# A two-layer mixture-of-experts backbone: experts in a pipelined order, their weights in longer runs, and a reordered routing chain

## Chip, cores and metric

One core of a Trainium2 chip runs the whole program in one launch. The metric is the device time of that launch in microseconds (us), as the median of several runs. TensorE is PE in the profile, VectorE DVE, ScalarE ACT, GpSimd POOL, SyncE SP; SP issues the weight transfers.

## What is computed

Two layers over 256 latent and 256 context tokens of 1024 channels, all in f32. Each layer has a token mixer (differential attention, a long convolution called hyena, windowed attention; gated and merged) and then a mixture of 16 experts in which every expert chooses its tokens:

```python
def moe(h, p):                     # h: (B, L, D), per sequence
    aff = softmax(h @ router_w)    # over the 16 experts
    g, idx = top_k(aff.T, CAP)     # each expert takes its CAP = 2 * 256 / 16 = 32 best tokens
    xe = gather(h, idx)            # (E, CAP, D)
    a = silu(xe @ moe_w1[e]) * (xe @ moe_w3[e])
    y = a @ moe_w2[e]              # all three 1024 x 1024
    return scatter_add(g * y, idx)
```

In layer 0 latent and context tokens are two sequences (64 rows to an expert); layer 1 needs the latent ones alone (32 rows). h is a normalized x, scaled and shifted per channel by values that the conditioning vector gives (`mod`, vectors 3 and 4 here). Each layer reads 3 x 16 x 4 MB = 201 MB of expert weights, once.

## The kernel before

Stages follow one another: mixer of layer 0 (about 60 to 950 us), routing, experts of layer 0 (1030 to 1515), mixer of layer 1 (1545 to 2145), routing, experts of layer 1 (2165 to 2621), final norm.

**Foreground and background.** `run_blocks` issues a list of projection blocks; each block's matmuls are the foreground. What follows from them (attention heads, hyena, filter, modulation, router, `post`) are generators, called tasks, kept by `self.bg`, a planner with a model of the engines' time. It steps tasks between foreground matmuls, by rough costs and due times, and `drain` or `force` run them without foreground. `yield wait(..., gate=...)` holds a task until its gate is true; `self.room(a2=2)` is a gate that asks for two dead buffers of the tag a2 (8 buffers of 2 KB to a partition). Allocating a tile of a full tag makes the engines wait for its old readers.

**Routing** (`post` for each of 8 channel tiles k, then `body` in `moe`). `post` transposes xT tile by tile to token rows and splits them into three bf16 parts xr[0], xr[1], xr[2] (through the difference tile xd), and accumulates the router's logits. Then come the softmax aff, four rounds of MAX and MATCH_REPLACE on a copy wk of its transpose, the mask's running count (mt, mb16), and `select(g)`, which builds one-hot matrices S for a group of 4 experts. `gather(g)` makes the experts' inputs xg out of S and xr in four steps of 24 matmuls; R is the row norm spread over the partitions; mod[:, 4] and mod[:, 3] scale and shift.

**Experts.** The weights come in 96 chunks of 2 MB for each layer, 6 to an expert (w1, w3, w2, two halves each), into 6 or 7 large buffers and a few smaller ones ahead of time. `fill(room)` (line 1622) issues as many as there is room for, on SP; `prod` (line 1786) calls it whenever it has used up a chunk (4 of the 8 k-steps; a k-step is 2 matmuls in layer 0, 4 in layer 1). `expert(e)` (line 1800) runs its three products one after the other: a = x w1, SiLU to s1, b = x w3, s1 = s1 * b, then transposes of s1 to aT, then y = aT w2. Into the k-steps `aside()` mixes steps of the side queue (gather and back of the next group, scatter of the last) and `bg.pump` background tasks. In layer 0 after expert 4 the room falls to 4 chunks, since layer 1's hyena filter takes buffers. PSUM has 5 banks of tag b and 2 of tag d (y).

In chunks, partition p holds rows p, 128 + p, ...: `v = A[n][l, e].rearrange("(k p) n -> p k n", p=128)`, a run of 4 KB for each row.

## Time and profile before

| | us |
|---|---|
| runs (3), median | 2635.15 |
| lowest and highest run | 2632.49, 2641.01 |
| the profiled execution, its time | 2637.57 |
| the profiled execution, its span | 2635.8 |

Busy in that span: PE 2232.3 us (85%), DVE 1334.5 (51%), ACT 883.4 (34%), POOL 790.4 (30%). 590.31 MB were moved, 224 GB/s on the mean. A window view gives for each stretch the span's busy time by engine, the granted clock of PE, the busy share of the 16 DMA engines (packets that overlap can take it over 1) and GB/s. In a row of a group view the time after the bar is idle time of that engine just before the group's instructions, and the releaser that ended most of it.

### The profile page before, as it was taken

The page shows a single profiled execution, that of the slowest core. Times are in us where ns is not written, and L with a number is a line of the kernel's source. Part 1 is how long each engine was busy: PE and PEld are TensorE (multiplying, and loading weights), DVE is VectorE, ACT ScalarE, POOL GpSimd, SP SyncE. Part 2 cuts the span into 40 slices and gives each one's busy share as a digit, 9 for nine tenths or more (in the row PEclk, how much of TensorE's full clock was granted, in tenths as well). Part 3 has the DMA queues.
Part 4 walks back from the last instruction along what each step waited for, and adds up shares of the span by engine and source line. Part 5 has one row for each costly group of instructions (what it writes and reads, how often), then busy time and mean ns, then how long its engine had stood idle before and what let it go on. Part 6 is the DMA issues. An engine that isn't in the chain of part 4 may idle for free.

```text
span 2635.8 us, 38658 instructions
## 1 busy us (share of the span) xinstructions
PE 2232.3 (85%) x14938; PEld 1528.6 (58%) x14938; DVE 1334.5 (51%) x2899; ACT 883.4 (34%) x1933; POOL 790.4 (30%) x775
## 2 busy tenths in 40 slices
PE   6999898989989998998999799889888886656565
PEld 4777666767768774333343277777777763222223
DVE  4777778787672324223442068777888541111111
ACT  4445344555452242101110055545545330000001
POOL 2643435532233530001110055564554420000000
PEclk8999999999999999999999999999999988888887
DMA  8444333121213367999999953332466789999997
GB/s 292 118 118 120 93 102 114 49 59 55 64 57 95 90 247 306 373 402 404 357 376 405 400 171 89 97 88 73 118 181 190 192 309 409 409 409 409 408 409 302
DMA packets 390239, 590.31 MB, mean 224 GB/s; under 512 B 45948, under 2 KB 278056, under 8 KB 388776
## 3 DMA queue, kind: packets, MB, share of 16 engines
q1 hardware_dynamic: 390056, 587.84, 62.8%
q8 instruction: 118, 1.93, 0.3%
q14 instruction: 65, 0.53, 0.1%
HBM read 584.66 MB, written 3.15 MB: 223 GB/s over the span
## 4 chain that ended last, share of the span: by engine, by line
PE 51%; DVE 19%; DMA 19%; issue 4%; ACT 4%; SPq 2%; POOL 1%; DVEq 0%; ACTq 0%; POOLq 0%
PE p L458 47%; DMA mw<-in_moe_w_dram 16%; DVE arena L261 6%; DVE t L261 5%; PE p L469 3%; DVE wl L261 2%; SPq L261 2%; DMA wm<-in_w_mod_dram 2%; DVE qp L261 1%; ACT arena L261 1%; ACT wh L261 1%; DVE yb L261 1%; DVE yc L261 1%; DVE ma L261 1%; POOL wl L261 1%
## 5 line engine op out<-in xcount | busy, mean ns | idle before, releaser
L458 PE MATMUL p<-mw,xg 128*32 128x256 f32 (+1 forms) x3072 | 403.3, 508 | 120.5 <-DMA mw<-in_moe_w_dram 120.0
L458 PE MATMUL p<-hhi,wl 128*128 128x512 f32 (+1 forms) x1344 | 480.6, 358 | 28.0 <-DVE wl L261 27.7
L458 PE MATMUL p<-hhi,wh 128*128 128x512 f32 (+1 forms) x1344 | 496.0, 369 | 6.4 <-ACT wh L261 3.3
L458 PE MATMUL p<-hlo,wh 128*128 128x512 f32 (+1 forms) x1344 | 476.6, 355 | 2.5 <-POOL hlo L261 1.3
L261 POOL TENSOR_TENSOR wl<-wraw,wh 128x512 fp32r<-128x512 f32 x232 | 342.4, 1476 | 417.5 <-ACT wh L261 344.8
L458 PEld LDWEIGHTS p<-mw,xg 128*32 128x32 f32 (+1 forms) x3072 | 136.3, 131 | 329.6 <-issue 205.4
L458 PEld LDWEIGHTS p<-hhi,wl 128*128 128x128 f32 x1344 | 258.4, 192 | 76.1 <-DVE wl L261 41.7
L458 PEld LDWEIGHTS p<-hhi,wh 128*128 128x128 f32 x1344 | 259.4, 193 | 43.6 <-issue 10.1
L458 PEld LDWEIGHTS p<-hlo,wh 128*128 128x128 f32 x1344 | 259.6, 193 | 29.5 <-POOL hlo L261 1.9
L261 ACT ACTIVATE wh<-wraw 128x1024 fp32r<-128x1024 f32 x232 | 242.3, 1053 | 54.0 <-DMA wraw<-in_w_in_dram 14.7
L458 PE MATMUL p<-mw,aT 128*32 128x256 f32 (+3 forms) x1760 | 199.5, 469 | 67.8 <-DMA mw<-in_moe_w_dram 51.6
L261 DVE TENSOR_TENSOR wl<-wraw,wh 128x512 fp32r<-128x512 f32 x231 | 196.2, 850 | 79.4 <-ACT wh L261 73.9
L261 ACT ACTIVATE arena<-p 128x512 f32<-128x512 f32 (+1 forms) x212 | 106.7, 506 | 383.0 <-PE p L458 304.9
L261 ACT ACTIVATE yS<-p 32x256 f32<-32x256 f32 (+2 forms) x84 | 35.2, 419 | 497.3 <-PE p L458 463.8
L458 PE MATMUL p<-yb,wh 128*128 128x512 f32 (+1 forms) x768 | 197.3, 347 | 1.4 <-ACT wh L261 1.2
L261 POOL TENSOR_TENSOR sq<-sq,sq 128x512 f32<-128x512 f32 (+1 forms) x6 | 6.3, 1058 | 575.6 <-ACT sq L261 573.3
L458 PEld LDWEIGHTS p<-mw,aT 128*32 128x32 f32 (+1 forms) x1760 | 77.1, 131 | 172.9 <-issue 92.7
L261 DVE TENSOR_TENSOR s<-s,p 128x512 f32<-128x512 f32 (+1 forms) x32 | 17.7, 554 | 287.6 <-PE p L458 287.4
L261 DVE COPY yS<-p 32x512 f32<-32x512 f32 (+1 forms) x60 | 33.3, 556 | 247.1 <-ACT yS L261 247.1
L458 PE MATMUL p<-yb,wl 128*128 128x512 f32 (+1 forms) x384 | 133.3, 347 | 22.5 <-DVE wl L261 21.6
L458 PEld LDWEIGHTS p<-yb,wh 128*128 128x128 f32 x768 | 133.3, 194 | 17.3 <-ACT wh L261 1.4
L261 ACT ACTIVATE arena<-p,t 128x512 f32<-128x512 f32 (+1 forms) x192 | 116.3, 612 | 50.9 <-DVE t L261 45.7
(235 smaller groups left out, 3489.7 us busy)
## 6 DMA issues: line engine op xcount, KB each, us to landing
mw<-in_moe_w_dram SPq DMA_DIRECT2D x173, 2048.0 KB, 19.5
wraw<-in_w_in_dram SPq DMA_DIRECT2D x152, 512.0 KB, 3.9
wm<-in_w_mod_dram SPq DMA_DIRECT2D x72, 512.0 KB, 4.7
mw<-in_moe_w_dram SPq DMA_DIRECT2D x40, 512.0 KB, 15.8
mw<-in_moe_w_dram SPq DMA_DIRECT2D x17, 1024.0 KB, 22.4
wraw<-in_w_branch_dram SPq DMA_DIRECT2D x32, 512.0 KB, 3.9
wm<-in_w_mod_dram SPq DMA_DIRECT2D x5, 2048.0 KB, 7.7
wraw<-in_w_in_dram SPq DMA_DIRECT2D x32, 256.0 KB, 3.3
```

Of the source, the lines that this page charges most:

```text
L261: return f(*args, **kw)
L458: self.nc.tensor.matmul(out, lhsT=lhsT, rhs=rhs, start=start, stop=stop, skip_group_check=tiles > 1)
L469: self.nc.tensor.transpose(out, in_, self.ident[:n, :n])
```

## The change

**Chunks.** w1 and w3 now give partition p the rows 8p to 8p + 7, so that half a matrix is a run of 16 KB to a partition; w2 gives it nf neighbouring rows in each part (nf = 4 in layer 0: 16 KB, nf = 2 in layer 1: 8 KB). The extra chunks that fill small buffers keep runs of 4 KB, twelve later chunks of layer 1 are split into one run of 8 KB and two of 4 KB, and the last expert's w2 stays as it was. To match, `post` writes xr with its columns permuted (channel 8p + k to place 128k + p in the gather's order), s1 is transposed with stride nf, and `router_prep` permutes vectors 3 and 4 of mod by 8 matmuls against selections of the identity matrix.

**Order of experts.** The chunk order is (0,w1), (0,w3), then for each e: (e+1,w1), (e,w2), (e+1,w3). `into(e, n)` is a first or second product, `turned(e)` the transposes and aT, `outof(e)` the third product. `turned(e)` is called in the middle of the next expert's first product.

**Routing.** The last `post` hands its xd, xr[1], xr[2] to `self.rest`, called behind the normalization of aff; MAX reads the transpose in PSUM (no copy wk); the cast to mb16 comes ahead of mt; the matmuls and the copy of R come ahead of the gather of k = 1; after two of the four gather steps of group 0 the first product begins, with the other two steps between its k-steps. Gather and back of the next group are queued one expert earlier.

**Gates.** Waits of filter and router get gates on a2; `clear(n)` forces background until n buffers of a2 are dead; hyena's uh and ul are allocated a step earlier, and yc once for two.

```diff
@@ router_prep
         if v == 4:
-            yield wait(self.modc[l][:, 4])
+            yield wait(self.modc[l][:, 4], gate=self.room(a2=2))
             self.router_prep(l)
...
+        m = self.modc[l][:, 3:5]
+        p = self.bank([128, KT, 2 * KT * 2])
+        for hf in range(2):
+            sw = self.sb("a2", [128, 4, KT, 16], name="sw")
+            self.vcopy(sw, self.ident.rearrange("p (q c) -> p c q", c=KT)[:, hf * 4:hf * 4 + 4, None, :].to_broadcast([128, 4, KT, 16]))
+            for c in range(4):
+                self.mm(p[:, hf * 4 + c], sw[:, c].rearrange("p k q -> p (k q)"), m.rearrange("p v k s -> p (v k s)"), True, True)
...
+        nc.vector.reduce_sum(own, self.ident.rearrange("p (k q) -> p k q", k=KT), axis=AX.X)
...
+        nc.vector.reduce_sum(m.rearrange("p v c s -> p c v s"), t.rearrange("p (c v) k s -> p c v s k", v=2), axis=AX.X)
@@ filter
-            yield wait(ab[0])
+            yield wait(ab[0], gate=self.room(a2=1))
...
-                yield wait(w3, dec) if j else wait()
+                yield wait(w3, dec) if j else wait(gate=self.room(a2=1))
...
+    def clear(self, n):
+        while self.model.dead("a2", BUFS["a2"]) < n:
+            self.bg.force()
@@ post
-        self.acopy(xr[0], p)
-        self.tt(d, p, xr[0], OP.subtract)
-        self.acopy(xr[1], d)
-        self.tt(xr[2], d, xr[1], OP.subtract, self.nc.gpsimd)
+        self.acopy(xr[0], pv)
+
+        def rest():
+            self.tt(d, pv, xr[0], OP.subtract)
+            self.acopy(xr[1], d)
+            self.tt(xr[2], d, xr[1], OP.subtract, self.nc.gpsimd)
+
+        if k < KT - 1:
+            rest()
+        else:
+            self.rest = rest
@@ moe
         for e in range(NE):
-            for n in ("moe_w1", "moe_w3", "moe_w2"):
-                v = A[n][l, e].rearrange("(k p) n -> p k n", p=128)
...
+            order += [(e + 1, 0), (e, 2), (e + 1, 1)] if e < NE - 1 else [(e, 2)]
...
+                        v = A[n][l, e].rearrange("(c p j) n -> p c j n", p=128, j=nf)
+                        chunks.append(v[:, hf * NC // 2:(hf + 1) * NC // 2])
+                else:
+                    chunks.append(A[n][l, e].rearrange("(p k) n -> p k n", p=128)[:, hf * 4:hf * 4 + 4, :])
...
             self.tt(aff, aff, mb, OP.mult)
+            self.rest()
...
-            wk = self.sb("a1", [E2, 256], name="wk")
-            self.vcopy(wk, p[0:E2])
+            wk = p[0:E2]
...
-            def prod(out, st, ws, free=True):
+            def prod(out, st, ws, free=True, mid=None):
...
-                    if k % SIDE or not aside():
+                    if mid and k == 4:
+                        mid()
+                    elif k % SIDE or not aside():
                         self.bg.pump(0.25)
...
+            def into(e, n, mid=None):
                 g, j = divmod(e, 4)
                 a = self.bank([128, N])
-                prod(a, st, w[0:2])
-                s1 = self.sb("a2", [128, N], name="s1")
-                nc.scalar.activation(s1, a, AF.Silu)
-                b = self.bank([128, N])
...
+                prod(a, lambda k: xg[g][k // 4][:, k % 4, j, :], weights(e, n), mid=mid)
...
+            def turned(e):
+                s1 = s1s.pop(e)
                 p = self.bank([128, nf, 128])
                 for f in range(nf):
-                    self.tr(p[:, f], s1[:, f * 128:(f + 1) * 128])
...
+                    self.tr(p[:, f], s1[:, f::nf] if e < NE - 1 else s1[:, f * 128:(f + 1) * 128])
...
-            finish(gather(0))
+            side.append(gather(0))
+            for _ in range(2):
+                aside()
+            into(0, 0)
...
-                if j == 2 and g < 3:
+                if j == 1 and g < 3:
                     side += [gather(g + 1), back(g + 1)]
...
-                expert(e)
+                into(e, 1)
+                if e < NE - 1:
+                    if j == 3:
+                        while aside():
+                            pass
+                    into(e + 1, 0, lambda: turned(e))
+                else:
+                    turned(e)
+                outof(e)
```

**What this moves.** First DVE, in the routing of layer 0, from the softmax (t is a small tile, aff the affinities) to the first MATCH_REPLACE. Before:

```order
L261 SCALAR_TENSOR_TENSOR t_8783<-t_8804,t_8802 128x4
L261 TENSOR_TENSOR xd_8774<-p_8767,xr_8373 128x512
L261 SCALAR_TENSOR_TENSOR aff_403<-p_8816,t_8783,cr_2951 128x16 x2
L261 SCALAR_TENSOR_TENSOR aff_403<-p_8817,t_8783,cr_2951 128x16 x2
L261 TENSOR_REDUCE t_8826<-aff_403 128x4
L261 TENSOR_TENSOR aff_403<-aff_403,t_8826 128x64
L261 TENSOR_REDUCE t_8826<-aff_403 128x4
L261 RECIPROCAL t_8826<-t_8826 128x4
L261 TENSOR_TENSOR aff_403<-aff_403,t_8826 128x64
L261 COPY wk_8866<-p_8863 32x256
L261 MAX t_8868<-wk_8866 32x8
L261 MATCH_REPLACE wk_8870<-t_8868,wk_8866 32x256
```

And after:

```order
L261 SCALAR_TENSOR_TENSOR t_8793<-t_8814,t_8812 128x4
L261 SCALAR_TENSOR_TENSOR aff_403<-p_8823,t_8793,cr_2977 128x16 x2
L261 SCALAR_TENSOR_TENSOR aff_403<-p_8824,t_8793,cr_2977 128x16 x2
L261 TENSOR_REDUCE t_8833<-aff_403 128x4
L261 TENSOR_TENSOR aff_403<-aff_403,t_8833 128x64
L261 TENSOR_REDUCE t_8833<-aff_403 128x4
L261 RECIPROCAL t_8833<-t_8833 128x4
L261 TENSOR_TENSOR aff_403<-aff_403,t_8833 128x64
L261 TENSOR_TENSOR xd_8784<-p_8777,xr_8383 128x512
L261 MAX t_8876<-p_8873 32x8
L261 MATCH_REPLACE wk_8878<-t_8876,p_8873 32x256
```

The difference xd went from ahead of the affinities to behind them, and the copy wk is gone.

Then PE, in layer 0's experts: products of expert 0 up to its third one (p is the PSUM bank, mw a chunk, xg the gathered input, s the s1 of the text). Before:

```order
L458 MATMUL p_9090<-mw_8402,xg_8935 64x512 x8
L458 MATMUL p_9090<-mw_8455,xg_8936 64x512 x8
L458 MATMUL p_9113<-mw_8508,xg_8935 64x512 x8
L458 MATMUL p_9113<-mw_8561,xg_8936 64x512 x8
L469 MATMUL p_9135<-cst_68,s_1499_9111 128x128 x4
L458 MATMUL p_9142<-mw_8904,aT_9140 64x512 x2
L458 MATMUL p_9142<-mw_8905,aT_9140 64x512 x2
L458 MATMUL p_9142<-mw_8906,aT_9140 64x512 x2
L458 MATMUL p_9142<-mw_8907,aT_9140 64x512 x2
L458 MATMUL p_9142<-mw_8912,aT_9140 64x512 x8
```

And after, from expert 0's second product on:

```order
L458 MATMUL p_9121<-mw_8518,xg_8943 64x512 x8
L458 MATMUL p_9121<-mw_8571,xg_8944 64x512 x8
L458 MATMUL p_9143<-mw_8912,xg_8943 64x512 x2
L458 MATMUL p_9143<-mw_8913,xg_8943 64x512 x2
L458 MATMUL p_9143<-mw_8914,xg_8943 64x512 x2
L458 MATMUL p_9143<-mw_8915,xg_8943 64x512 x2
L458 MATMUL p_9143<-mw_8920,xg_8944 64x512 x2
L469 MATMUL p_9154<-cst_68,s_1495_9107 128x128 x4
L458 MATMUL p_9143<-mw_8920,xg_8944 64x512 x6
L458 MATMUL p_9171<-mw_8922,aT_9159 64x512 x8
```

p_9143 is expert 1's first product: the transposes of expert 0's s1 went into its middle, with ten of its matmuls ahead of them and six behind.

## Rows read from the trace of the kernel before

**Rows 1.** The page's busy times, and GB/s in its 40 slices.
```profile
PE 2232.3 (85%) x14938; PEld 1528.6 (58%) x14938; DVE 1334.5 (51%) x2899; ACT 883.4 (34%) x1933; POOL 790.4 (30%) x775
...
GB/s 292 118 118 120 93 102 114 49 59 55 64 57 95 90 247 306 373 402 404 357 376 405 400 171 89 97 88 73 118 181 190 192 309 409 409 409 409 408 409 302
```

**Rows 2.** Windows: length, PE, PEld, DVE, ACT, POOL busy; PEclk, DMA, GB/s.
```profile
60.00:950.00 890.00, 833.31 (x4508) 645.20 (x4507) 596.12 (x1300) 402.80 (x881) 384.90 (x382) 0.98 0.31 91
1030.00:1510.00 480.00, 426.18 (x2132) 163.19 (x2128) 136.57 (x310) 58.44 (x130) 36.68 (x65) 0.99 0.99 387
2170.00:2605.00 435.00, 265.10 (x3107) 121.31 (x3099) 49.75 (x126) 25.38 (x70) 0.00 (x0) 0.84 1.03 409
```

**Rows 3.** The page's chain that ended last, by line.
```profile
PE p L458 47%; DMA mw<-in_moe_w_dram 16%; DVE arena L261 6%; DVE t L261 5%; PE p L469 3%; DVE wl L261 2%; SPq L261 2%; DMA wm<-in_w_mod_dram 2%; DVE qp L261 1%; ACT arena L261 1%; ACT wh L261 1%; DVE yb L261 1%; DVE yc L261 1%; DVE ma L261 1%; POOL wl L261 1%
```

**Rows 4.** Windows in transfers: 8 KB loads, 16 KB spill, its reload, 4 KB expert weights.
```profile
18.00:20.00 2.00, 1.15 (x2) 0.30 (x2) 1.86 (x6) 0.00 (x0) 0.00 (x0) 0.93 0.99 411
46.50:47.50 1.00, 1.00 (x5) 0.82 (x4) 1.00 (x3) 1.00 (x3) 0.60 (x1) 0.74 1.07 459
945.00:946.00 1.00, 1.00 (x6) 0.84 (x5) 0.00 (x0) 0.00 (x0) 0.00 (x0) 1.00 1.13 477
2300.00:2400.00 100.00, 64.22 (x702) 29.12 (x691) 13.78 (x35) 6.16 (x17) 0.00 (x0) 0.83 1.03 409
```

**Rows 5.** Windows around the first product of each layer's experts.
```profile
1025.00:1030.00 5.00, 5.00 (x62) 3.48 (x61) 4.79 (x21) 4.70 (x16) 0.00 (x0) 1.00 0.14 48
1030.00:1035.00 5.00, 5.00 (x26) 1.71 (x24) 1.47 (x8) 0.01 (x1) 0.00 (x0) 1.00 0.38 130
2160.00:2165.00 5.00, 5.00 (x59) 4.75 (x60) 2.67 (x9) 1.92 (x6) 0.00 (x0) 0.67 0.10 42
2165.00:2170.00 5.00, 5.00 (x100) 3.00 (x94) 1.57 (x8) 2.41 (x5) 0.00 (x0) 1.00 0.42 127
```

**Rows 6.** Windows in layer 0's experts, in the order of time.
```profile
1037.00:1105.00 68.00, 59.32 (x348) 23.47 (x346) 15.69 (x38) 8.66 (x22) 0.00 (x0) 1.00 0.97 375
1105.00:1180.00 75.00, 71.71 (x324) 25.38 (x320) 13.90 (x26) 5.31 (x9) 0.00 (x0) 1.00 1.02 409
1180.00:1430.00 250.00, 224.26 (x1148) 91.17 (x1146) 97.66 (x226) 37.27 (x88) 36.68 (x65) 0.98 0.99 382
1430.00:1505.00 75.00, 60.06 (x274) 19.48 (x271) 6.88 (x10) 5.31 (x9) 0.00 (x0) 1.00 1.03 408
```

**Rows 7.** Groups of PE, 1180 to 1430 us: busy, mean ns, idle before.
```profile
L458 PE MATMUL p<-mw,xg 128*64 128x512 f32 x452 | 109.4, 604 | 1.7 <-DMA mw<-in_moe_w_dram 1.7
L458 PE MATMUL p<-mw,aT 128*64 128x512 f32 x236 | 58.1, 641 | 6.3 <-DVE aT L261 6.3
...
L469 PE MATMUL p<-cst,s 128*128 128x128 f32 x32 | 5.2, 284 | 11.8 <-DVE s L261 11.8
```

**Rows 8.** Timeline of layer 0's routing: start, duration (us), instruction, idle before.
```profile
1009.05 0.69 DVE L261 TENSOR_TENSOR xd<-p,xr 128x512 f32<-128x512 f32 x1
...
1010.34 0.22 DVE L261 TENSOR_REDUCE t<-aff 128x4 f32<-128x64 f32 x1
...
1013.40 0.41 DVE L261 COPY wk<-p 32x256 f32<-32x256 f32 x1 [0.68 <-PE p L469]
...
1023.70 4.18 PE L458 MATMUL p<-S,xr 128*128 128x128 bf16 x72
1023.97 0.42 DVE L261 COPY R<-p 128x256 f32<-128x256 f32 x1 [2.88 <-PE p L458]
```

**Rows 9.** Timeline of layer 1's routing, DVE.
```profile
2150.01 0.42 DVE L261 TENSOR_TENSOR xd<-p,xr 128x256 f32<-128x256 f32 x1
...
2153.35 0.41 DVE L261 COPY wk<-p 16x256 f32<-16x256 f32 x1 [0.77 <-PE p L469]
```

**Rows 10.** Instructions on wr (min/median/max ns), and the window with layer 1's router.
```profile
L458 PE MATMUL p<-wr,mod x48: 177/262/376, 320.4 to 2024.4; 128*128 128x16 f32 x48
...
2020.00:2045.00 25.00, 19.86 (x181) 15.54 (x179) 21.36 (x56) 14.51 (x37) 5.18 (x7) 1.00 0.31 85
```

More of the change, by code (lines that the diff above doesn't have):

```diff
@@ L813, in router_prep @@
         self.gw[l], self.cr[l] = gw, cr
+        m = self.modc[l][:, 3:5]
[5 more added lines that the diff above has]
+                self.mm(p[:, hf * 4 + c], sw[:, c].rearrange("p k q -> p (k q)"), m.rearrange("p v k s -> p (v k s)"), True, True)
+        own = self.tiny(KT)
+        nc = self.nc
+        nc.vector.reduce_sum(own, self.ident.rearrange("p (k q) -> p k q", k=KT), axis=AX.X)
+        t = self.sb("a1", [128, KT * 2, KT, 2], name="mp")
+        self.tt(t, p.rearrange("p c (v k s) -> p (c v) k s", v=2, k=KT), own[:, None, :, None].to_broadcast([128, KT * 2, KT, 2]), OP.mult)
+        nc.vector.reduce_sum(m.rearrange("p v c s -> p c v s"), t.rearrange("p (c v) k s -> p c v s k", v=2), axis=AX.X)
     def dft_load(self, slots, j0=0):
@@ L1259, in hyena_gen @@
         yield wait(uv, gate=lambda: l in self.K and len(self.dft or ()) == 2 and self.room(a2=2)())
+        uh = self.sb("a2", [128, 2, ns * 128], F32R, name="uh")
+        ul = self.sb("a2", [128, 2, ns * 128], F32R, name="ul")
         p = self.bank([128, 2, ns, 128])
@@ L1486, in ev_sk @@
                 def ev_sk(p, g=g):
+                    self.clear(1)
                     r = self.sb("a2", [128, 512], name="sk")
@@ L1580, in post @@
             self.mm(self.acc[32 * s:32 * s + NE], self.gw[l][:, s, k], xT[:, k, s * 256:(s + 1) * 256], k == 0, k == KT - 1, ns)
-        xr = [x[:, :, z] for x in self.xr]
-        d = self.sb("a2", [128, nq, 128], name="xd")
+        xr = [x.rearrange("p i (c q) -> p i c q", c=KT)[:, :, :, k * 16:(k + 1) * 16] for x in self.xr]
+        d = self.sb("a2", [128, nq, KT, 16], name="xd")
+        pv = p.rearrange("p i (q c) -> p i c q", c=KT)
         sq = self.sb("a1", [128, 128], name="sq")
@@ L1608, in moe @@
         chunks = []
+        order = [(0, 0), (0, 1)]
         for e in range(NE):
-            for n in ("moe_w1", "moe_w3", "moe_w2"):
-                v = A[n][l, e].rearrange("(k p) n -> p k n", p=128)
-                for hf in range(2):
-                    if e == NE - 1 and n == "moe_w2":
-                        chunks.append(v[:, :, hf * 512:hf * 512 + 512])
-                    else:
-                        chunks.append(v[:, hf * 4:hf * 4 + 4, :])
+            order += [(e + 1, 0), (e, 2), (e + 1, 1)] if e < NE - 1 else [(e, 2)]
+        at = {o: 2 * i for i, o in enumerate(order)}
+        for e, n in order:
+            n = ("moe_w1", "moe_w3", "moe_w2")[n]
+            for hf in range(2):
+                if n == "moe_w2":
+                    if e == NE - 1:
+                        chunks.append(A[n][l, e].rearrange("(k p) n -> p k n", p=128)[:, :, hf * 512:hf * 512 + 512])
+                    else:
+                        v = A[n][l, e].rearrange("(c p j) n -> p c j n", p=128, j=nf)
+                        chunks.append(v[:, hf * NC // 2:(hf + 1) * NC // 2])
+                else:
+                    chunks.append(A[n][l, e].rearrange("(p k) n -> p k n", p=128)[:, hf * 4:hf * 4 + 4, :])
         self.mw = []
@@ L1620, in moe, with row, load @@
         extra = {4: (4, 0, 1), 7: (3, 2, 2)} if l < L - 1 else {5: (4, 0, 1), 7: (3, 2, 2)}
+        def row(c, k):
+            return c[:, k] if len(c.shape) == 3 else c[:, k // c.shape[2], k % c.shape[2]]
+        def load(t, c):
+            if len(c.shape) == 4:
+                t = t.rearrange("p (c j) n -> p c j n", j=c.shape[2])
+            nc.sync.dma_start(t, c)
         def fill(room, more=0):
@@ L1682, in body @@
             self.tt(aff, aff, mb, OP.mult)
+            self.rest()
+            self.rest = None
             xr = self.xr
@@ L1734, in gather @@
                         k = k2 * 2 + kk
+                        if k == 1:
+                            pr = self.bank([128, ns, 128])
+                            for s in range(ns):
+                                for i in range(2):
+                                    self.mm(pr[:, s], self.ones, sr[:, s * 2 + i], i == 0, i == 1)
+                            R = self.sb("a2", [128, ns, 128], name="R")
+                            self.vcopy(R, pr)
                         for s in range(ns):
@@ L1739, in gather @@
                                             i == 0 and h == 0, i == 1 and h == 2)
-                    if k2 == 0:
-                        pr = self.bank([128, ns, 128])
-                        for s in range(ns):
-                            for i in range(2):
-                                self.mm(pr[:, s], self.ones, sr[:, s * 2 + i], i == 0, i == 1)
-                        R = self.sb("a2", [128, ns, 128], name="R")
-                        self.vcopy(R, pr)
                     for kk in range(2):
@@ L1821, in expert @@
                     y = self.bank([128, n], "d")
-                    w = self.mw[6 * e + 4:6 * e + 6]
+                    w = weights(e, 2)
                     if np_ > 1:
```

41 lines of the change are left out of this document (22 added, 19 removed).

## The prediction

> **What bounds the kernel now.** I read the page's slices and busy times first, then windows by stage, then the chain. PE is busy 85% of the span, but the two expert stages look different from the rest: the slices from 14 on and from 32 on carry 306 to 409 GB/s, the mixers between them about 50 to 300 [rows 1]. By stages [rows 2]: in the layer-0 mixer (60 to 950 us) PE is busy 833 of 890 us and the DMA share is 0.31, so PE sets it; the experts of layer 0 have PE 426 of 480 us and the DMA at 0.99, so the two bounds nearly coincide; the experts of layer 1 have PE 265 of 435 us and the DMA at 1.03 and 409 GB/s, so the weights' transfer alone sets them. The chain agrees: expert weights (mw) are 16% of it [rows 3].
>
> So two things can shorten the expert stages: bytes per us, and, where PE shares the bound, its waits.
>
> **1. Longer runs.** Before, a 2 MB chunk (2.097 MB, 96 to a layer) is read in runs of 4 KB, after it of 16 KB (layer 0, and w1/w3 of layer 1) or 8 KB (w2 of layer 1). Four places show a rate by run length [rows 4]: weights of 4 KB 409 GB/s at share 1.03; the modulation weights, 8 KB, 411 at 0.99; a spill of 16 KB runs 459 at 1.07; its reload, with some short packets in it, 477 at 1.13. For each unit of share that is 397, 415, 429 and 422. At the 1.03 of the saturated stage I take 428 GB/s for 16 KB and 420 for 8 KB, with 415 as lower bound for both and 442 and 427 as upper ones (429 and 415 times 1.03): I stay under these because the last two windows are 1 us long each, the 8 KB one 2 us, and none of them is a saturated stage. A chunk then costs 4.900 or 4.993 us for 5.127.
>
> *Layer 1.* Of its 96 chunks 9 are on their way before the first buffer comes free and 87 follow at the bound: 49 of 16 KB x 0.227 = 11.1, 24 of 8 KB x 0.134 = 3.2, 12 split ones (half 8 KB, half 4 KB) x 0.067 = 0.8, the last two unchanged: **-15.1**. At the bounds: 415 gives -6, 442 and 427 give -25.
>
> *Layer 0, where the DMA binds* [rows 6]: 1105 to 1180 and 1430 to 1505 run at 409 and 408. 150 us x (1 - 409/428) = **-6.7**. In the first of them PE is busy 71.7 of 75 us, which leaves it just the 3.3 us that are taken.
>
> The Trainium skill ("DMA: Bandwidth & Descriptors", Specifications) gives 512 B as the smallest transfer for line rate, by which 4 KB runs are at line rate already and this part would be worth nothing. The four windows differ by 5 to 8% at equal share, so here the trace speaks against it, if on few microseconds; what the rule would make of the time is rival A.
>
> **2. Pipelined experts.** Before, the transposes of s and the copy aT stand between an expert's second and third product, with PE waiting; after, they stand in the middle of the next expert's first product. From 1180 to 1430 us PE is idle 25.7 of 250 us at 382 GB/s [rows 6]. By groups [rows 7], 11.8 us of that are the wait for DVE's s, 6.3 for DVE's aT, 1.7 for weights. I take all 18.1 of s and aT away: there are 8 hand-overs (32 transposes, 4 each), so 1.5 us of waiting for s and 0.8 for aT at each. After, five k-steps, thus 10 matmuls of 109.4/452 = 0.24 us, stand ahead of the transposes and three behind them: 2.4 us of cover for 1.5, and 1.5 for 0.8. What is late next: PE's own work, 224.3 + the remaining idle 5.9 = 230; and the transfer, 250 x 382 = 95.5 MB at 428 = 223, plus 6.8 us that the share of 0.99 holds beside the weights (240.3 at full share, less 95.5/409 = 233.5) = 230. Two bounds of 230 that meet don't run without friction; with 4 us of it, 234: **-16** (floor -20). Without longer runs the transfer would need 240.3.
>
> From 1037 to 1105 us [rows 6]: 25.5 MB at 428 = 59.6, PE 59.3. Floor -8.4; a piece of the gather still stands there, and the DMA is restarting, so **-5** (0 to -8.4).
>
> The strided columns for the transposes (s1 with stride nf) I cost at nothing: 32 transposes are 5.2 us busy [rows 7]; if a strided read doubled them, +5.2 in that stretch.
>
> **3. Routing chain.** The DMA stands still from the time the slots are full until the first product frees one: 48 GB/s at 1025 to 1030, 130 at 1030 to 1035; in layer 1 42 and 127 [rows 5]. What delays the first product delays the whole train of weights. Out of the chain go, in layer 0, xd 0.69 and the wk copy 0.41 (the MAX reads PSUM) [rows 8]; in layer 1 0.42 and 0.41 [rows 9]. R, which waited 2.88 us behind 72 gather matmuls, comes ahead of most of them [rows 8]. Against it, half of the gather's 96 matmuls (48 x 4.18/72 = 2.8 us) stand now between the first k-steps, still ahead of the fourth, which frees the first chunk: moved, but not out of the DMA's way. And the rest of the last post (xd, two copies) is not gone, only behind the affinities, where it competes with the MAX chain. Net I take **-1.2** in layer 0 (0 to -3) and **-1** in layer 1 (0 to -2): the direct savings, little more.
>
> **4. Added work for the permuted columns.** router_prep gets two 128x512 copies, 8 matmuls, a multiplication and two reductions. The nearest rows are the 0.69 of a 128x512 tensor operation, 0.22 of the small reduce [rows 8] and 0.18 to 0.26 of a matmul [rows 10]: DVE about 2 x 0.69 + 0.4 + 2 x 0.3 = 2.4, PE 8 x 0.2 = 1.6. In layer 0 it is background work. In layer 1 it stands at about 2023 us, where DVE is busy 21.4 of 25 us [rows 10] and the last drain of the mixer follows: **+2.5** there (0 to +4).
>
> **5. Gates.** Waiting tasks of filter, router and hyena are held until buffers of the tag a2 (2 KB to a partition) are free, and two places force the background on until they are. This moves no work off or onto an engine; it puts layer 0's filter and hyena steps some 30 to 60 foreground matmuls later. They drain at the same blocks, PE has 57 us idle there in 890 [rows 2]: **0, between -8 and +8**. Layer 1's mixer keeps its order.
>
> **Sum.** Layer 0: -6.7 - 16 - 5 - 1.2 = -28.9. Layer 1: -15.1 - 1 + 2.5 = -13.6. Together -42.5. The profiled execution took 2637.6 (span 2635.8), so 2595.1; it lies 2.4 over the median of the runs, 2635.15, so **2592.7 us** for the median.
>
> **Rivals.**
> *A. The run length changes nothing*, and the transfer stays at 409. For it: the windows of [rows 4] are short, and two of them are other kinds of traffic (one a write). Against it: all three long ones are 5 to 8% higher per share. Then layer 0 between 1180 and 1430 stops at 240.3 (-9.7), 1037 to 1105 at perhaps 64 (25.5/409 = 62.3 and friction; -4), routing -1.2, layer 1 -1 + 2.5: -13.4, **2621.8**. Chance 0.12.
> *B. New waits take the place of the old ones.* The transposes need s1, which needs a product and the SiLU; if DVE or ACT is late by more than five k-steps (filter and gather run beside them: DVE 97.7 us in 250), or if PSUM buffers run out with one more product open, PE waits as before. For it: the wait for s was 1.5 us on the mean with 2.4 of cover, so a hand-over 0.9 us longer than the mean shows again. Against it: what shows then is the rest of a wait, not the whole. If all of it came back, only the longer runs would count in layer 0, where PE allows: 250 less the 1.7 of weight waits, -2; -5 at the two bound stretches, -1 ahead of them, routing -1.2, layer 1 -13.6: -22.8, **2612.4**. Chance 0.12.
> *C. Both floors are reached*: 442 and 427 GB/s and no friction. 1105 to 1180 loses the 3.3 that PE leaves, 1430 to 1505 75 x (1 - 409/442) = 5.6, the middle 20, 1037 to 1105 PE's idle 8.7, routing 3; layer 1 -25 - 2 + 0: -67.6, **2567.6**. Chance 0.13.
> *D. Slower.* The layer-0 mixer: the gates hold the filter until the foreground has passed its due blocks, and the drain ahead of the first branch block then runs filter and hyena steps with nothing of PE's beside them. To be slower by over 8 us it must bring over 50 us of new PE idle between 60 and 950 us, where there are 57 now, thus nearly double them; with 70 more, **2663**. For it: these steps move by tens of matmuls; against it: they still come ahead of the same block. Chance 0.03.
> *E. It doesn't do what it says*: SP's issue order or the free order of buffers binds the transfer, and expert waits go over into waits for weights: so that only routing and router count (-1.2 - 1 + 2.5): **2635.5**. Chance 0.03.
>
> **How the numbers follow.** Forecast 0.57, A 0.12, B 0.12, C 0.13, D and E 0.03 each. The forecast's own range is 2578 to 2606 (the rate bounds of layer 1 are -10 and +9, the mixer's -8 and +8). The range takes in A to C, and 3 us of the mixer's uncertainty beyond: 2564 to 2624. A measurement of this kernel tells a difference from none from about 0.3%, 8 us: faster 0.94 (forecast, A, B, C), same 0.03 (E), slower 0.03 (D).
>
> **What would show it.** Longer runs: the window of 2300 to 2400 us reads about 428 GB/s instead of 409 at the same share; at 409 step 1 is wrong and A holds. Pipelining: the group of transposes from s no longer waits on DVE, and the middle of layer 0's experts takes about 234 us for the same bytes; if the idle shows under other names (PSUM, a busy DVE), B holds. Routing: the first product starts about 1 us sooner from the last post. Router: a cluster of about 2.4 us on DVE, and the layer-1 mixer longer by as much. Gates: the layer-0 mixer within 8 us of its old length. The forecast is wrong if a mixer stage moves by more than that.

## Result and profile after

The changed kernel takes 2602.24 us (median of 4 runs, 2598.70 to 2604.44), the kernel before on the same chip 2637.41: a ratio of 0.9867, 95% interval 0.9845 to 0.9889, or 35 us. Predicted were 2592.7 (2564 to 2624). Repeated in a later run it gave 0.9870 (0.9852 to 0.9888). So it is faster, by somewhat less than forecast; but the sum hides errors that cancel. To see them, cut the two profiled executions (2637.57 and 2600.63 us) into stages with a few landmarks: the copy of the router's logits (lg) in each layer, the first matmul of a first product (mw with xg), the last start of a third product (mw with aT), the first matmul of layer 1's router weights (wr; at 2022.8 us before, at 1993.3 after). The landmarks of after, from the views of instructions on these tiles (min/median/max ns, first and last start; mw for each layer apart):

```profile
L261 DVE COPY lg<-p x3: 412/413/417, 993.9 to 2125.4; 16x256 f32<-16x256 f32 x3
...
L458 PE MATMUL p<-mw,xg x1024: 592/592/1116, 1012.3 to 1478.9; 128*64 128x512 f32 x171
L458 PE MATMUL p<-mw,aT x544: 379/592/644, 1037.0 to 1492.9; 128*64 128x512 f32 x160, 128*64 128x256 f32 x22
...
L458 PE MATMUL p<-mw,xg x2048: 376/379/637, 2140.5 to 2574.3; 128*32 128x256 f32 x187
L458 PE MATMUL p<-mw,aT x1216: 216/379/636, 2153.4 to 2585.6; 128*32 128x256 f32 x138, 128*32 128x64 f32 x36
```

| stage, us | before | after | difference | predicted | after, repeated |
|---|---|---|---|---|---|
| start to logits, layer 0 (mixer) | 1005.4 | 993.9 | -11.5 | 0 (-8 to +8) | 996.0 |
| logits to first product (routing) | 22.4 | 18.4 | -4.0 | -1.2 | 18.4 |
| experts, layer 0 | 493.7 | 480.6 | -13.1 | -27.7 | 479.3 |
| to the router weights of layer 1 | 501.3 | 500.4 | -0.9 | 0 | 501.6 |
| router to logits, layer 1 | 124.4 | 132.0 | +7.6 | +2.5 | 132.2 |
| logits to first product, layer 1 | 17.4 | 15.1 | -2.3 | -1 | 15.1 |
| experts, layer 1 | 458.2 | 445.1 | -13.1 | -15.1 | 444.6 |

The last column is a second execution of the changed kernel (after_again): a stage repeats within about 2 us. The rest (the tail) is +0.4.

The page's rate and the chain by line of after, to be held against [rows 1] and [rows 3]:

```profile
GB/s 296 117 126 115 98 114 106 65 57 50 58 57 90 98 251 304 366 427 414 396 408 391 398 145 83 112 82 74 121 180 187 174 297 410 425 424 422 423 424 304
...
PE p L458 48%; DMA mw<-in_moe_w_dram 20%; DVE arena L261 6%; DVE t L261 4%; PE p L469 3%; DVE wl L261 2%; DMA wm<-in_w_mod_dram 2%; DVE qp L261 1%; SPq L261 1%; DVE yb L261 1%; ACT wh L261 1%; ACT arena L261 1%; DVE ma L261 1%; DVE yc L261 1%; ACT qp L261 1%
```

Layer 1's slices went from 409 to 424, and the weights' share of the chain from 16 to 20%, though they come faster: more of PE's waits are now for them. The windows that answer to [rows 4] and [rows 6] (length; PE, PEld, DVE, ACT, POOL busy; PEclk, DMA share, GB/s):

```profile
2300.00:2400.00 100.00, 65.27 (x732) 28.60 (x724) 13.25 (x34) 6.17 (x17) 0.00 (x0) 0.84 1.01 423
1025.00:1090.00 65.00, 62.58 (x354) 24.74 (x350) 14.81 (x37) 8.66 (x22) 0.00 (x0) 0.97 0.89 366
1090.00:1160.00 70.00, 66.27 (x288) 24.00 (x287) 13.44 (x26) 4.73 (x8) 0.00 (x0) 0.98 1.01 427
1160.00:1400.00 240.00, 223.75 (x1154) 89.74 (x1155) 87.05 (x200) 35.38 (x83) 28.25 (x50) 1.00 1.00 409
1400.00:1475.00 75.00, 64.70 (x288) 22.89 (x286) 18.75 (x38) 7.82 (x15) 8.53 (x16) 0.98 0.97 392
```

At 16 KB the saturated transfer does 427 GB/s (428 taken), in layer 1's mix 423. But in layer 0 it comes to that rate in one of these windows only (409 GB/s at a share of 1.00 in the longest): at 1025 to 1090 PE is busy 62.6 of 65 us and the share falls to 0.89. PE's waits in layer 0's experts, before (1027.8 to 1521) and then after (1012.3 to 1493): us in total, times, longest.

```profile
PE p L469 <- DVE s L261: 18.7, 16, 2.7
PE p L458 <- DMA mw<-in_moe_w_dram: 13.3, 10, 1.7
PE p L458 <- DVE aT L261: 12.6, 16, 0.9
PE p L458 <- POOL hx L261: 3.9, 4, 1.4
PE p L469 <- DVE sg L261: 2.7, 4, 2.2
PE p L458 <- DVE sr L261: 2.5, 2, 1.2
```

```profile
PE p L458 <- DMA mw<-in_moe_w_dram: 20.6, 21, 2.0
PE p L458 <- POOL hx L261: 6.4, 4, 3.5
PE p L458 <- DVE sr L261: 3.5, 2, 1.8
PE p L469 <- DVE sg L261: 2.9, 4, 2.2
PE p L469 <- DVE s L261: 0.9, 1, 0.9
PE p L458 <- DVE aT L261: 0.8, 1, 0.8
```

The hand-over waits went from 31.3 us to 1.7, as forecast. 7 us of them came back as waits for weights, and PE itself became busier; the windows of the whole stage, before and after:

```profile
1027.80:1521.00 493.20, 438.44 (x2216) 170.95 (x2216) 142.64 (x327) 65.30 (x146) 38.97 (x67) 0.99 0.99 384
```

```profile
1012.30:1493.00 480.70, 444.97 (x2270) 176.32 (x2268) 145.44 (x335) 67.74 (x153) 39.62 (x68) 0.99 0.97 395
```

PE 438.4 to 445.0, of which some 3 us are the gather's 48 matmuls that now stand behind the first product.

### The profile page after: what moved, and what is told of

The parts are those of the page before. It is cut to its first block, busy times and chain, and to the rows that moved or that the text cites. A ratio compares the mean times of both kernels' runs of the same rounds, so it can differ in the third digit from the quotient of the medians.

```text
span 2598.8 us, 38727 instructions
## 1 busy us (share of the span) xinstructions
PE 2244.1 (86%) x14970; PEld 1539.4 (59%) x14970; DVE 1338.3 (51%) x2907; ACT 884.2 (34%) x1933; POOL 793.6 (31%) x775
## 4 chain that ended last, share of the span: by engine, by line
PE 51%; DMA 22%; DVE 18%; ACT 3%; issue 3%; POOL 1%; SPq 1%; DVEq 0%; ACTq 0%; POOLq 0%
PE p L458 48%; DMA mw<-in_moe_w_dram 20%; DVE arena L261 6%; DVE t L261 4%; PE p L469 3%; DVE wl L261 2%; DMA wm<-in_w_mod_dram 2%; DVE qp L261 1%; SPq L261 1%; DVE yb L261 1%; ACT wh L261 1%; ACT arena L261 1%; DVE ma L261 1%; DVE yc L261 1%; ACT qp L261 1%
## 5 line engine op out<-in xcount | busy, mean ns | idle before, releaser
L458 PE MATMUL p<-mw,xg 128*32 128x256 f32 (+1 forms) x3072 | 412.4, 509 | 116.4 <-DMA mw<-in_moe_w_dram 114.0
L261 ACT ACTIVATE wh<-wraw 128x1024 fp32r<-128x1024 f32 x232 | 242.4, 1053 | 50.8 <-DMA wraw<-in_w_in_dram 14.6
L261 ACT ACTIVATE s<-p 128x512 f32<-128x512 f32 (+1 forms) x32 | 15.7, 491 | 344.1 <-PE p L458 344.0
```

What stands on the lines that cost most here:

```text
L261: return f(*args, **kw)
L458: self.nc.tensor.matmul(out, lhsT=lhsT, rhs=rhs, start=start, stop=stop, skip_group_check=tiles > 1)
```

## Experiments

All were timed against the kernel before on the same chip; ratios have 95% intervals.

| kernel | median us | before | ratio |
|---|---|---|---|
| gates_only | 2647.88 | 2639.30 | 1.0032 (1.0021 to 1.0042) |
| gates_noclear | 2627.10 | 2642.24 | 0.9950 (0.9935 to 0.9965) |
| runs_gates | 2620.34 | 2639.30 | 0.9926 (0.9912 to 0.9940) |
| short_runs | 2646.14 | 2639.30 | 1.0026 (1.0013 to 1.0038) |
| short_dummy | 2633.73 | 2639.56 | 0.9977 (0.9967 to 0.9988) |
| serial_experts | 2621.62 | 2639.30 | 0.9927 (0.9914 to 0.9941) |
| old_routing | 2608.41 | 2639.56 | 0.9881 (0.9866 to 0.9897) |
| no_perm_l1 | 2602.08 | 2639.56 | 0.9857 (0.9840 to 0.9873) |
| spread | 2593.80 | 2639.56 | 0.9824 (0.9809 to 0.9840) |
| spread3 | 2608.79 | 2642.24 | 0.9878 (0.9859 to 0.9897) |
| both | 2620.86 | 2642.24 | 0.9928 (0.9911 to 0.9945) |
| after_again | 2606.81 | 2642.24 | 0.9870 (0.9852 to 0.9888) |

Their stages, by the same landmarks (us):

| kernel | mixer 0 | routing 0 | experts 0 | router to logits 1 | experts 1 |
|---|---|---|---|---|---|
| before | 1005.4 | 22.4 | 493.7 | 124.4 | 458.2 |
| gates_only | 1018.9 | 22.4 | 486.7 | 125.9 | 457.9 |
| gates_noclear | 997.6 | 22.1 | 489.0 | 125.4 | 457.8 |
| runs_gates | 997.9 | 22.2 | 493.3 | 128.9 | 443.3 |
| short_runs | 1017.3 | 18.7 | 492.1 | 126.7 | 460.9 |
| short_dummy | 996.5 | 18.8 | 492.8 | 132.6 | 459.8 |
| serial_experts | 1000.2 | 18.3 | 495.9 | 132.2 | 444.9 |
| old_routing | 996.6 | 22.4 | 478.4 | 133.5 | 443.2 |
| no_perm_l1 | 997.9 | 18.5 | 480.5 | 127.2 | 448.0 |
| spread | 996.5 | 18.5 | 468.7 | 132.2 | 444.8 |
| spread3 | 996.8 | 18.5 | 481.9 | 131.2 | 443.8 |
| both | 1025.0 | 18.8 | 469.6 | 132.5 | 445.1 |
| after | 993.9 | 18.4 | 480.6 | 132.0 | 445.1 |

### Which part carries the gain

**gates_only**: before, with the gates, `clear`, the earlier uh and ul and the shared yc (two of the places shown).

```diff
+                        self.clear(2)
                         self.svt = [self.sb("a2", [128, 4, 128], name="svt") for _ in range(2)]
...
-            yield wait(ab[0])
+            yield wait(ab[0], gate=self.room(a2=1))
```

> The kernel before with the gates, clear(), the earlier uh/ul and the shared yc alone. Theory (the gates shortened the layer-0 mixer, 11.5 us between the profiles of before and after): the wait of PE for yd and arena falls as in after, the last router logits of layer 0 come near 994 us instead of 1005, everything behind keeps its length: about 2626 us. Rival (the 11.5 us come from another part of the change or from the execution): 2637 us, the logits at 1005.

Neither held: the layer-0 mixer became 13.5 us longer. The reason is below, under the mixer. But layer 0's experts became 7.0 us shorter (4.7 in gates_noclear, below), though the edit doesn't touch them: PE waits 15.4 us for s there instead of 18.7, and is busy 435.6 us instead of 438.4. So part of what the whole change gains in that stage comes with the gates.

**runs_gates**: gates_only with the longer runs and their permutations.

```diff
-                v = A[n][l, e].rearrange("(k p) n -> p k n", p=128)
+                        chunks.append(A[n][l, e].rearrange("(p k) n -> p k n", p=128)[:, hf * 4:hf * 4 + 4, :])
```

> The kernel before with the gates and the longer runs (permuted xr, mod and s1 included), experts serial and routing chain as before. Theory (the runs are worth the transfer's bound wherever it binds, and the buffers carry PE's hand-overs): 427 GB/s in 1105-1180 us and in layer 1; layer 1's experts 445 us from first to last product instead of 458, layer 0's 480 to 484 instead of 494, layer 1's mixer +7 for the permutation in router_prep, mixer of layer 0 -11: about 2609 us. Rival (in layer 0 the hand-overs bind and longer runs give only their 5 us in the two saturated windows): layer 0's experts 488, about 2615 us.

Layer 1's experts fall to 443.3 us: the runs alone carry that whole term. Layer 0's experts don't gain at all (493.3, against 493.7 before and 486.7 in gates_only), which neither the theory nor the rival had. PE's groups with aT and the transposes (busy, mean ns, idle before) and the window of the stage tell why; first those of gates_only, then those of runs_gates and its wait for weights:

```profile
1041.30:1528.00 486.70, 435.62 (x2220) 170.64 (x2220) 143.30 (x327) 65.20 (x146) 39.46 (x68) 1.00 1.00 389
```

```profile
L458 PE MATMUL p<-mw,aT 128*64 128x512 f32 x480 | 108.5, 603 | 12.5 <-DVE aT L261 11.8 <-DMA mw<-in_moe_w_dram 0.6
...
L469 PE MATMUL p<-cst,s 128*128 128x128 f32 x64 | 10.5, 286 | 15.4 <-DVE s L261 15.4
```

```profile
1020.10:1513.00 492.90, 445.93 (x2218) 174.87 (x2218) 142.95 (x327) 65.29 (x146) 39.26 (x67) 0.98 0.95 384
```

```profile
L458 PE MATMUL p<-mw,aT 128*64 128x512 f32 x480 | 116.0, 637 | 11.9 <-DVE aT L261 11.8
...
L469 PE MATMUL p<-cst,s 128*128 128x128 f32 x64 | 12.3, 316 | 15.4 <-DVE s L261 15.4
```

```profile
PE p L458 <- DMA mw<-in_moe_w_dram: 7.7, 7, 1.3
```

The waits for weights fall (7.7 us; 13.3 in before), and the transfer now idles (share 0.95): PE with its hand-overs sets the pace. For the same instructions PE is 10 us longer busy, 7.5 of it in the third products, which stand right behind the hand-over waits. The granted clock of the stage is 0.98 in place of 1.00, so for a small part of it PE was at the lower of its two levels, 1.2 GHz.

**short_runs**: after, with the old chunk rows and columns.

```diff
-                    chunks.append(A[n][l, e].rearrange("(p k) n -> p k n", p=128)[:, hf * 4:hf * 4 + 4, :])
+                    chunks.append(A[n][l, e].rearrange("(k p) n -> p k n", p=128)[:, hf * 4:hf * 4 + 4, :])
```

> The kernel after with the old chunk rows (4 KB runs), and without the permutations of xr, mod and s1 that go with them. Theory (the runs carry layer 1's 13 us and most of layer 0's): 409 GB/s, layer 1's experts 458 us, layer 0's 487 to 491, layer 1's mixer 7 us shorter than in after: about 2615 us. Rival of the prediction's arithmetic (pipelining alone is worth the removed waits, 14 us between 1037 and 1430): layer 0's experts 480 us, about 2607 us.

Experts 492.1 and 460.9: the theory's side. That it is slower than before in all is the layer-0 mixer's 1017.3 once more.

**short_dummy**: short_runs with the permutation's instructions, their result unread (the branch under `if False` never runs).

```diff
-        nc.vector.reduce_sum(m.rearrange("p v c s -> p c v s"), t.rearrange("p (c v) k s -> p c v s k", v=2), axis=AX.X)
+        dm = self.tiny(32, F32) if False else self.sb("a1", [128, 2, KT, 2], name="dm")
+        nc.vector.reduce_sum(dm.rearrange("p v c s -> p c v s"), t.rearrange("p (c v) k s -> p c v s k", v=2), axis=AX.X)
```

> short_runs with router_prep's permutation left in as work, its result written to a tile that nobody reads; rows of 4 KB and unpermuted columns as in short_runs. Theory (the layer-0 mixer of gates_only and short_runs is 23 us longer than that of after because clear(2) has to force 11 background steps there in place of 7, and what differs is only the order that the planner gives with or without the permutation's instructions): last router logits of layer 0 at 992 to 998 us instead of 1017, layer 1's mixer 3 to 5 us longer, experts as in short_runs (492, 461): about 2627 us. Rival (the chunk rows or the permuted columns themselves set the mixer's length): 1017 us and 2648 us.

The mixer is back at 996.5 us, as the theory had it; the total is 2633.7 rather than 2627 (the profiled execution, with a span of 2628.4, was one of the faster). Its window in layer 1 and PE's waits for weights in layer 0's experts (1010 to 1503 us):

```profile
2300.00:2400.00 100.00, 58.81 (x646) 25.70 (x638) 8.89 (x20) 3.77 (x10) 0.00 (x0) 0.84 1.03 409
```

```profile
PE p L458 <- DMA mw<-in_moe_w_dram: 33.0, 25, 2.6
```

Without the hand-overs, but at 409 GB/s, PE waits 33 us for weights in layer 0.

**serial_experts**: after, with each expert's three products one behind the other.

```diff
-            order += [(e + 1, 0), (e, 2), (e + 1, 1)] if e < NE - 1 else [(e, 2)]
+        order = [(e, n) for e in range(NE) for n in range(3)]
...
-                    into(e + 1, 0, lambda: turned(e))
-                else:
-                    turned(e)
+                aside()
+                turned(e)
```

> The kernel after with the products of each expert one behind the other again (chunk order w1, w3, w2), all else as in after. Theory (with faster transfers PE is as much a bound as the DMA in layer 0, and part of its 30 us of hand-over waits shows): layer 0's experts 486 to 490 us instead of 481, layer 1's 446: about 2610 us. Rival 1 (the buffers hide the hand-overs in full): 2602 us. Rival 2 (all the waits come back): layer 0's experts 505 us, about 2627 us.

495.9 us, above the theory's 490 and below the second rival's 505: 15 of 30 us show. In total it is 0.6% slower than after. So layer 0's experts take 487 to 494 us in serial order with 4 KB runs, 493 and 496 with longer runs alone, 492 and 493 with the pipelined order alone, and 481 and 479 with both. Either part by itself only exchanges one bound for the other. Against the kernels that have the gates alone (486.7 and 489.0) either part even costs 3 to 9 us, and both together gain 6 to 10. In short_runs, short_dummy and serial_experts some 2 us of that cost are, by old_routing below, the gather matmuls that were moved into the stage.

### Where the rest of layer 0's gain went

**spread**: after with one number changed.

```diff
-SIDE = 2
+SIDE = 4
```

> The kernel after with SIDE = 4 in place of 2: steps of gather, back and scatter every fourth k-step instead of every second. Theory (in layer 0 PE's waits for weights, 20.6 us, come from bursts: two experts of 35 us with all side work, in which the slots fill up, then two of 21 to 25 us that outrun the transfer): the experts even out to 27 to 33 us, the waits fall by 5 to 8 us, layer 0's experts 474 to 476 us instead of 481: about 2596 us. Rival (the waits come from the room of 4 chunks beside the filter, or the transfer's average): 481 us, 2602 us.

It gained more than the theory allowed: 468.7 us, and a total of 2593.8, below both kernels. The stage's window and the wait for weights (1011 to 1485 us):

```profile
1011.00:1485.00 474.00, 447.27 (x2311) 179.04 (x2309) 147.55 (x340) 69.32 (x158) 40.74 (x68) 0.99 0.98 405
```

```profile
PE p L458 <- DMA mw<-in_moe_w_dram: 10.5, 11, 1.3
```

The wait for weights halves, from 20.6 to 10.5 us. From the start of one third product to the next, experts 8 to 12 took 34.8, 28.2, 28.1 and 36.9 us in after and 30.9, 33.5, 28.6 and 31.2 in spread.

**spread3**: SIDE = 3.

> The kernel after with SIDE = 3. An expert's three products then have 9 places for side steps, against 11 in after and 5 in spread (SIDE = 4). Theory (what spread gained in layer 0's experts, 481 to 469 us, is the evening out of bursts of 13 side steps over the experts): 9 places are nearly as dense as 11, so 477 to 480 us, about 2600 us. Rival (the gain has to do with which k-step the side steps stand at, beside the transposes at k = 4): as spread, 469 to 471 us, about 2593 us.

481.9 us, nearer to the theory of bursts (477 to 480) than to the rival: with 9 places for an expert the 13 side steps still fall on one expert and a half. The place at k = 4, which the transposes take in after, isn't what matters.

### The layer-0 mixer

**gates_noclear**: gates_only without the two calls of `clear`.

```diff
-                        self.clear(2)
...
-                    self.clear(1)
```

> gates_only without the calls of clear, so that no background is forced ahead of the windowed attention's tiles. Theory (the 11 forced steps cost gates_only its time): PE works through at 527 to 561 us, logits of layer 0 at 990 to 1000 us instead of 1019, about 2622 us. Rival (the gates themselves hold the tasks back, and the drain pays for it later): logits at 1010 us or more, 2636 us or more.

As the theory has it: 2627.1 us, logits at 997.6. Windows of gates_only, then of gates_noclear:

```profile
530.00:540.00 10.00, 5.84 (x17) 3.49 (x17) 9.29 (x21) 6.84 (x18) 5.83 (x7) 0.57 0.06 19
540.00:550.00 10.00, 6.50 (x31) 5.32 (x31) 8.47 (x33) 4.53 (x16) 0.00 (x0) 0.67 0.00 0
550.00:560.00 10.00, 7.16 (x58) 6.04 (x57) 4.44 (x13) 4.92 (x10) 2.85 (x4) 0.84 0.00 1
```

```profile
530.00:540.00 10.00, 10.00 (x47) 8.33 (x46) 6.61 (x15) 6.07 (x17) 3.23 (x6) 1.00 0.05 10
540.00:550.00 10.00, 8.78 (x43) 6.91 (x41) 9.10 (x27) 5.51 (x13) 5.95 (x5) 1.00 0.18 52
```

In gates_only PE has no projection matmul at all from 527.5 to 561.2 us (from 540 on the DMA, which feeds those, stands at 0): `clear(2)` forces 11 background steps in the order as it is built, attention's and hyena's, most of them waiting for DVE; PE is idle a third of the time and the clock falls as far as 0.57. In after, runs_gates and short_dummy it is 7 steps, and these cost nothing that shows: the mixer takes 994 to 1000 us in the kernels with 7, and 997.6 here with none. So it matters which steps are forced, and not only how many; the four that make the difference weren't told apart. The rest of the gates is a gain: without `clear`, 7.8 us in the mixer against before. (After without `clear` wasn't run.)

**both**: spread, and the permutation's selection tiles written by POOL ahead of time.

```diff
-            self.vcopy(sw, self.ident.rearrange("p (q c) -> p c q", c=KT)[:, hf * 4:hf * 4 + 4, None, :].to_broadcast([128, 4, KT, 16]))
+            sw = self.sw[hf]
...
+                self.tt(self.sw[hf], b, b, OP.mult, self.nc.gpsimd)
```

> spread (SIDE = 4) with the selection tiles sw made by POOL ahead of the wait for the modulation vector, and the small mask computed once, so that DVE has 1.4 us less to do in layer 1's router. This moves the planner's order in layer 0: clear(2) forces 11 background steps again, as in gates_only and short_runs, in place of 7. Theory (the number of forced steps sets the layer-0 mixer): logits of layer 0 at 1015 to 1020 us, layer 1's mixer 2 to 4 us shorter: about 2612 us. Rival (the 23 us of gates_only and short_runs had another cause, the missing permutation's own work): logits at 996 us, about 2590 us.

The edit touches 1.4 us of work, and the layer-0 mixer grows by 29 us against spread: 11 forced steps again, by the count of the order, and the profile has the same hole:

```profile
L261 DVE COPY lg<-p x3: 411/414/417, 1025.0 to 2146.5; 16x256 f32<-16x256 f32 x3
```

```profile
550.00:560.00 10.00, 6.08 (x50) 5.13 (x51) 6.03 (x18) 2.43 (x4) 2.46 (x3) 0.83 0.01 2
```

The saving in layer 1's router did not come (132.5 us, 132.2 in spread): these 1.4 us of DVE weren't what it cost.

### Routing and router

**old_routing**: after with the chain as before (xd ahead of the affinities, copy wk, mt first, R after the first step, gather in one piece).

```diff
-            side.append(gather(0))
-            for _ in range(2):
-                aside()
+            finish(gather(0))
```

> The kernel after with the routing chain and the gather of group 0 as before (xd and its copies ahead of the affinities, copy wk, mt first, R after the first two k, gather in one piece ahead of the first product). Theory: from the logits to the first product 22.4 us instead of 18.4 in layer 0 and 17.5 instead of 15.1 in layer 1, but 48 gather matmuls (2.8 us) leave layer 0's experts: +3.6 us, about 2605.5 us. Rival (the whole of both differences counts, since the first freed chunk comes later by that): +6.4 us, about 2608.5 us.

Stages: +4.0 and +2.2 in the two routings, -2.2 and -1.9 in the experts of both layers. In time the ratio is 0.9881 against 0.9867 and 0.9870 of after, 3 to 4 us; their intervals overlap, so that the time agrees with the theory's 3.6 but doesn't rule out the rival's 6.4.

**no_perm_l1**: no permutation in layer 1's router_prep.

```diff
         self.gw[l], self.cr[l] = gw, cr
+        if l:
+            return
```

> The kernel after without the permutation of mod in layer 1's router_prep (layer 1's gathered inputs are then scaled and shifted with another channel's values; the instructions behind it are the same). Theory (the permutation costs its 2.4 to 3 us on DVE and, by the clock that falls while PE waits for it, as much again on PE): layer 1's mixer 7 us shorter, about 2595 us. Rival of the prediction (its own 2.5 us and no more): 2599.5 us.

Router to logits fell by 4.8 us (127.2), more than a stage differs by between two executions. The total fell by 0.1% (0.9857 against 0.9867), within the intervals, with layer 1's experts 2.9 us longer in this profile; it neither supports 7 us nor excludes 2.5. What the permutation costs can be seen in the trace of after: the timeline of DVE, that of PE, the window behind them; and, last, the window at the same place of before:

```profile
1995.31 1.15 DVE L261 COPY sw<-cst 128x512 f32<-128x512 f32 x2
1996.37 0.28 DVE L261 TENSOR_REDUCE t<-cst 128x8 f32<-128x128 f32 x1
1998.46 0.42 DVE L261 TENSOR_TENSOR mp<-p,t 128x256 f32<-128x256 f32 x1 [1.81 <-PE p L458]
1998.92 0.42 DVE L261 TENSOR_REDUCE mod<-mp 128x32 f32<-128x256 f32 x1
```

```profile
1996.07 2.36 PE L458 MATMUL p<-mod,sw 128*128 128x32 f32 x16 [0.89 <-DVE sw L261]
```

```profile
1999.00:2008.00 9.00, 7.67 (x44) 5.59 (x44) 7.72 (x16) 2.26 (x5) 2.96 (x6) 0.52 0.35 117
```

```profile
2025.00:2034.00 9.00, 6.63 (x56) 4.35 (x54) 8.67 (x21) 3.80 (x10) 3.41 (x6) 1.00 0.37 118
```

DVE does 2.3 us of work (2.4 predicted), but waits 1.8 us in it for 8 matmuls that take 2.4 us on PE, where 1.6 had been taken. Behind it the clock is at 0.52, about its lower level, where it was 1.00 before: PE had waited 0.9 us and then run matmuls of 32 columns only. The attention's matmuls that follow take up to 0.78 us where they took 0.48 before. On the chain that ended last the cluster takes 4.0 us, from sw to mod. In the same 9 us, from 5.7 to 14.7 us behind the start of layer 1's first matmul on wr, the granted clock is 0.50 to 0.66 in all nine executions with the permutation and 1.00 in all five without it (before, gates_only, gates_noclear, short_runs, no_perm_l1).

The whole of the +7.6 isn't the permutation, though. Pairs of kernels give 3.0 us for it (gates_only to runs_gates, where the runs change too), 4.8 (no_perm_l1 to after) and 5.9 (short_runs to short_dummy), so at most 2 us are left for the clock behind the 4.0 of the cluster; they weren't measured apart. And short_runs and no_perm_l1, without the permutation, still take 126.7 and 127.2 us where before took 124.4: 2 to 3 us come from elsewhere (gates_only and gates_noclear have 1 to 1.5 of them), and why stays open.

## Why the prediction was right, and where its steps were off

**Rate by run length: right.** 427 GB/s at 16 KB where 428 were taken, 423 in layer 1's mix. Layer 1's term was -15.1 and came as -13.1 (-14.6 between gates_only and runs_gates). The rate per unit of share is 419 to 423 in these two windows, and the saturated share itself falls from 1.03 to 1.01: the step from 429 per share times 1.03 to an upper bound of 442 had no ground. Rival A fell: short_dummy (409) and after (423) differ in the rows and columns alone. The Trainium skill ("DMA: Bandwidth & Descriptors", Specifications) puts the smallest transfer for line rate at 512 B; here 4 KB still gave 4% less than 16 KB, and the measurement decides.

**Hand-overs and layer 0's experts: right in kind, too large.** The hand-over waits went from 31.3 to 1.7 us, but the stage gained 13.1 where 27.7 were said, and the gates alone bring 4.7 to 7.0 of the 13.1. Measured is, for the whole stage, a wait for weights of 20.6 us where 13.3 had been, 3.7 more for POOL and DVE (hx, sr and sg), and PE busy 6.6 us longer. The sum -29.6 + 7.3 + 3.7 + 6.6 is -12, against -13.1 by the landmarks.

The step that failed is that the stage was priced window by window, as if the other work in each stayed where it stood. The change itself moves it: gather and back are queued one expert earlier, and the background falls elsewhere. Cut after at the same number of the experts' matmuls as before, and the stretches said to gain 5, 3.3, 16 and 3.3 us changed by -5.8, +10.2, -28.3 and +7.5, and the one ahead of them by +3.2. Here are the second and the fourth of them, before and then after:

```profile
1105.40:1182.90 77.50, 72.58 (x328) 25.70 (x324) 15.28 (x28) 5.31 (x9) 0.00 (x0) 1.00 1.02 409
1430.10:1505.40 75.30, 60.36 (x274) 19.61 (x272) 6.88 (x10) 5.31 (x9) 0.00 (x0) 1.00 1.03 408
```

```profile
1087.30:1175.10 87.80, 82.35 (x432) 32.78 (x430) 19.82 (x45) 9.59 (x23) 0.00 (x0) 0.98 1.01 428
1393.90:1476.70 82.80, 71.64 (x321) 26.02 (x322) 21.17 (x43) 8.65 (x17) 9.27 (x18) 0.98 0.97 395
```

The transfer runs at 428 GB/s in the second, yet PE, which had 5 us to spare there, got about 10 us more to do: 96 gather matmuls came in from the middle. In the fourth PE got 11 us more, and the share falls to 0.97. These pieces of work come in bursts: the slots fill while PE is late, and then PE outruns the transfer. spread, which changes nothing but their spacing, took away half of the wait for weights and 12 us of the stage; at 468.7 us it is close to the 466.0 that the forecast's terms make, if with the gates' 5 to 7 us in it. The friction of 4 and 3.4 us that was put on the two middle bounds can't be read apart from this.

The strided transposes, costed at nothing, take 12.3 us in runs_gates and 10.5 in gates_only (11.9 in after and 10.7 in short_dummy): 1 to 2 us in the stage, the lower clock included.

**Rivals.** B was 2612: the old waits are gone, but a quarter of their time came back as waits for weights, which no rival had as bursts (E had the waits, as the whole of them). C was out of reach, since its rate was. Something near D's mechanism exists: background forced with little beside it in the layer-0 mixer, with 21 to 29 us, in gates_only, short_runs and both (each against its partner with 7 steps or none). It isn't the drain that D named but `clear`. The change as a whole escapes it by luck, by the order that the permutation's own instructions happen to give.

**Gates: wrong size.** 0 with 8 us to each side was said; it is -11.5 (-9.4 in the repetition), past the 8 us that the prediction itself named as the sign of a wrong forecast, and with other work in the router +11.9 to +19.6. The step that failed is the argument that tasks which drain at the same block cost the same: what counts is which steps are forced with nothing beside them, and that could have been seen in the order of the changed kernel, where `clear(2)` forces 7 or 11.

**Router: too small.** +2.5 (0 to +4) was said, and it is +7.6 between the profiles, of which 3 to 6 are the permutation. DVE's work was sized right (2.3 us for 2.4), but it stands in one chain with PE's matmuls, 4.0 us together, and the price of the lower clock behind it was left out. At least 2 of the 7.6 us aren't explained.

**Routing: about right on the net.** -2.2 was said for both layers as the net. The routings alone gained 6.3, but by old_routing some 2 us come back in the experts of each layer, as the prediction said of the moved gather; what is left is 2 us by the stages and 3 to 4 in time, near what can be told from none. In layer 0 the 48 matmuls moved account for 2.8 of 4.0.

That the total came near is in part luck: a mixer that gained 11 us unforeseen stood against layer 0's experts, which gained 15 less than forecast, and a router that cost 5 more. The forecast's own range, 2578 to 2606, is also narrower than the two bounds that it names for it make (-18 and +17, so 2575 to 2610).

## What to carry to other kernels

Where transfer and TensorE bound a stage almost equally, longer runs and a better overlap are worth nothing or less each and something together; test both in a two-by-two table before dropping either, on a base that has all the other edits (here the gates alone shortened the stage). Between two such bounds look at how side work is spread over the time that the buffers cover: evening it out was worth 12 us here, nearly as much as the whole pipelined order (15 in serial_experts). A window of the old trace prices a change only as long as the change leaves the other work in it where it is. In a kernel whose order comes from a planner, look after each edit at which steps are forced with nothing beside them, since an edit of 1.4 us can move them.
